# The even mixer's weight splits: low parts by an accumulating DMA onto a negated high part, instead of a VectorE subtract

## The chip, the core and the metric

The kernel runs on one core of one Trainium2 chip, as one program. The metric is the device time of one execution in microseconds (us); a lower time is better. All times here are of this one core. Engine names follow the profile: PE is TensorE (PEld its weight load), DVE VectorE, ACT ScalarE, POOL GpSimd, SP SyncE, which only issues DMAs here. A queue that an engine feeds with DMAs is written SPq, POOLq.

## The reference, cut to what matters

The program is a trunk of two layers over 512 tokens of width 1024, in fp32. Each layer is a half-step feed-forward, a mixer, an attention to 256 memory tokens and another half-step feed-forward, each followed by a layer norm. The mixer of layer 0, the even one, is what the change touches:

```python
def mixer_ab(h, w_in, w_out, q_gain, k_gain, sink, ang_2d, ang_1d):
    qa, ka, va, qb, kb, vb = jnp.split(h @ w_in, AB_SPLITS, axis=-1)   # w_in 1024 x 1536
    ...
    qa = apply_rope(rms_norm(qa, q_gain), ang_2d)
    ka = apply_rope(rms_norm(ka, k_gain), ang_2d)
    out_a = global_gqa(qa, ka, va)                       # 8 heads of 64, dense
    ...
    out_b = window_gqa_sink(qb, kb, vb, sink)            # 8 heads of 64, a band of +-128
    return jnp.concatenate([out_a, out_b], axis=-1) @ w_out            # w_out 1024 x 1024
```

The output is the (1, 512, 1024) fp32 trunk result.

## The kernel before, in words

**Products.** TensorE multiplies in fp32r, a rounded form of fp32. To keep fp32 accuracy each operand is held as two fp32r tiles: the high part is the rounded value, the low part is the value minus the high part. `mm3` (line 307) makes a product as high x high, high x low and low x high, three matmuls of 128x128 by up to 512 columns accumulated in one PSUM bank. So each weight needs a high and a low tile in SBUF before TensorE can use it.

**Weights.** `weights()` (line 313) loads up to 1 MB of fp32 weights into a `raw` buffer, of which there are two, over SyncE's DMA queue. It cuts the buffer in pieces of 128 x 1024 and for each takes two tiles of the tag `slab` (27 buffers in the kernel, shared with activations and everything else of that size). `split` (line 296) then has ScalarE copy the piece to the fp32r high tile (in the trace `ACT CAST slab<-raw`) and VectorE subtract the high tile from the piece into the low tile (`DVE TENSOR_TENSOR slab<-raw,slab`). The raw buffer comes free when both have read it.

**The even mixer** (`mixer_ab`, line 709) calls `weights()` through two helpers. `w_cols512` (line 344) fetches a group of 512 columns of `w_in` as two loads of 1 MB (512 rows each) with two pieces per load; a piece is two blocks of 128 rows by 512 columns. It is called for three groups in this order: columns 512 to 1023 (keys and values of the dense heads, half of the banded queries), 0 to 511 (dense queries) and 1024 to 1535 (the rest). That makes 12 pieces. `w_rows_pairs` (line 363) fetches rows of `w_out` for a pair of heads that lie 256 rows apart: a load has two sources, one for the lower 64 partitions and one for the upper 64. For the first half of the heads it loads half the columns at a time (4 loads with one piece each, in `half_rows`), and for the last four head pairs all columns (2 loads with two pieces each, just before `down`). That makes 8 pieces.

In time the mixer runs from about 328 us, when the first raw load is issued under the end of the first feed-forward, to about 600 us. Its stages are: layer norm of the input in four blocks of 128 tokens (VectorE, ScalarE, and on GpSimd the reciprocal root `lny`), the key and value projection (from 365 us), the query projections with RMS norm and rotary embedding (GpSimd makes the roots `rms8y`, `rms2y` and the rotary adds `slab<-t,t`), eight dense heads, eight banded heads, and the output projection, half of it mixed into the banded heads and the other half after them.

**The order of instructions.** Nearly every instruction is recorded as an operation by a `Recorder` (so nearly all carry line L143) and written out by a planner, `Graph.emit` (line 168). The planner keeps a clock per engine, gives each operation a modelled duration (`cost`, line 110), and always issues the operation that can start first; among the ready ones of an engine the one recorded first goes first. Two figures of it matter here: a GpSimd DMA is given 700 ns on its engine, and its result counts as there 4000 ns after that, plus 90 ns for any step between engines. Each engine then runs its instructions strictly in the written order. A tile's next user waits until the last reader of the buffer is done.

**An existing use of the same means.** In the feed-forward layers, `down_fast` (line 518) already makes some of its tiles by a GpSimd DMA that adds `ffn_w_down` rows from HBM onto a slab: 40 DMAs of 512 KB, in the page as `POOL DMA_DIRECT2D slab<-ffn_w_down x40`. They write plain fp32.

Of the kernel before, what the change touches and what calls it, by code (L numbers as in the profile page):

```python
# [16 lines left out]
AF = mybir.ActivationFunctionType  # L17
ALU = mybir.AluOpType
# [3 lines left out]
D = 1024  # L22
# [230 lines left out]
class Kernel:  # L253
# [56 lines left out]
        mm(ps, st[0], mv[1], start=False, stop=False, **kw)  # L310
        mm(ps, st[1], mv[0], start=False, stop=last, **kw)

    def weights(self, srcs, shape, pieces, between=None):

        nc = self.nc
        raw = self.tile(self.raw, [P, *shape], F32, "raw")
        for part, src in srcs:
            nc.sync.dma_start(out=part(raw), in_=src)
            if between:
                between()  # L320
                between = None
        got = []
        for piece in pieces:
            v = piece(raw)
            shp = list(v.shape)
            wh, wl = self.slab(F32R, shp), self.slab(F32R, shp)
            self.split(v, wh, wl)
            got.append((wh, wl))
        return got

# [13 lines left out]
    def w_cols512(self, w, c0):  # L344

        got = []
        for q in range(2):
            src = w[q * 512 : (q + 1) * 512, c0 : c0 + 512].rearrange("(k p) f -> p k f", p=P)
            got += self.weights(
                [(lambda r: r, src)], (4, 512), [lambda r, i=i: r[:, 2 * i : 2 * i + 2, :] for i in range(2)]  # L350
            )
        return got

# [9 lines left out]
    def w_rows_pairs(self, w, r0, c0=None):  # L363


        cols = slice(0, D) if c0 is None else slice(c0, c0 + 512)
        srcs = [
            (lambda r, s=s: r[64 * s : 64 * s + 64], w[r0 + 256 * s : r0 + 256 * s + P, cols].rearrange("(b p) f -> p b f", p=64))
            for s in range(2)
        ]  # L370
        if c0 is None:
            return self.weights(srcs, (2, D), [lambda r, i=i: r[:, i, :] for i in range(2)])
        return self.weights(srcs, (2, 512), [lambda r: r])[0]

    def rsqrt(self, sums, n, tag, mean, eps):

# [961 lines left out]
```

## Time and profile before

| | us |
|---|---|
| median of 3 runs | 2215.97 |
| lowest and highest of the 3 | 2215.14, 2216.75 |
| span of the profiled execution | 2218.7 |
| PE busy in it | 2185.8 (99%) |
| DVE busy in it | 1415.7 (64%) |
| ACT busy in it | 878.2 (40%) |
| POOL busy in it | 318.0 (14%) |

The profiled execution is one more run of the kernel; its span is 2.7 us longer than the median of the others. Rows of instructions read: start (us), duration (us), engine, line, operation, output tile <- inputs, size, count; a bracket at the end gives how long the engine had been idle before it and what released it. A row with a count stands for several instructions in a row. Rows of groups read: line, engine, operation, tiles, size, count, then busy us and mean ns of one, then the idle time before them and what ended it. An issue row of a DMA ends with the median time from issue to landing. GpSimd's DMA instruction is only the issue; the data lands later.

### The profile page before, as it was taken

Reading aid. Unit: us, or ns where it says so; the run is one execution under the profiler, and the core shown is the slowest. Engines: PE = TensorE matmul, PEld = TensorE weight load, DVE = VectorE, ACT = ScalarE, POOL = GpSimd, SP = SyncE. Lnnn points to the kernel's source line nnn. Section 1 sums busy time; section 2 is a strip of 40 time slices with the busy share of each in tenths; the row PEclk is TensorE's granted clock in tenths of the full one; section 3 lists DMA queues with packets and bytes.
Section 4 is the critical chain, followed back from the end, with each engine's and each line's share of the span. In section 5 each row is a group of like instructions: output and inputs, shape, how many; then the busy total and the mean of one; then the engine's idle time right before and its main releaser. Section 6 shows DMA issues by size and latency. Waiting matters only on the chain.

```text
span 2218.7 us, 28479 instructions
## 1 busy us (share of the span) xinstructions
PE 2185.8 (99%) x11264; PEld 1863.8 (84%) x11264; DVE 1415.7 (64%) x2127; ACT 878.2 (40%) x1412; POOL 318.0 (14%) x431
## 2 busy tenths in 40 slices
PE   8999999999999999999999999999999999999998
PEld 7888888778998988888888888888989989888886
DVE  5566657788745756655765566567767557566556
ACT  4333333466443433333333233245554434333331
POOL 0000022544000000000300001214330000000002
PEclk9999999999999999999999999999999999999999
DMA  7443333102442642334334444235553325433342
GB/s 222 143 142 120 106 107 104 39 10 70 130 133 96 182 135 95 95 121 149 120 105 131 143 142 147 95 102 148 141 157 124 124 96 161 124 100 93 111 152 67
DMA packets 195221, 265.15 MB, mean 120 GB/s; under 512 B 8848, under 2 KB 139536, under 8 KB 195088
## 3 DMA queue, kind: packets, MB, share of 16 engines
q1 hardware_dynamic: 181136, 231.88, 32.9%
q0 software_dynamic: 13952, 31.46, 6.6%
q8 instruction: 88, 1.44, 0.3%
q14 instruction: 45, 0.37, 0.1%
HBM read 248.63 MB, written 4.19 MB: 114 GB/s over the span
## 4 chain that ended last, share of the span: by engine, by line
PE 94%; DVE 3%; ACT 1%; POOL 1%; DMA 1%; issue 1%; SPq 0%; DVEq 0%; POOLq 0%; ACTq 0%
PE a L143 59%; PE d L143 21%; PE t L143 14%; DVE slab L143 1%; DVE t L143 1%; ACT slab L143 1%; DVE x L143 0%; POOL slab L143 0%; DMA raw<-ab_w_out 0%; ACT t L143 0%; DMA slab<-t 0%; POOL rms8y L143 0%; ACT junk L143 0%; DMA x<-x 0%; POOL lny L143 0%
## 5 line engine op out<-in xcount | busy, mean ns | idle before, releaser
L143 PE MATMUL a<-xh,slab 128*128 128x512 f32 (+1 forms) x2960 | 892.9, 382 | 0.0
L143 PEld LDWEIGHTS a<-xh,slab 128*128 128x128 f32 x2960 | 549.1, 188 | 106.8
L143 PE MATMUL a<-xl,slab 128*128 128x512 f32 (+1 forms) x1480 | 565.1, 382 | 0.0
L143 PE MATMUL d<-slab,slab 128*128 128x512 f32 (+2 forms) x1856 | 448.8, 381 | 3.3 <-ACT slab L143 3.3
L143 DVE TENSOR_TENSOR slab<-raw,slab 128x1024 fp32r<-128x1024 f32 x300 | 368.8, 1250 | 92.7 <-ACT slab L143 92.2
L143 PEld LDWEIGHTS d<-slab,slab 128*128 128x128 f32 x1856 | 334.5, 188 | 67.3 <-ACT slab L143 5.1
L143 ACT CAST slab<-raw 128x1024 fp32r<-128x1024 f32 x300 | 304.3, 1048 | 206.2 <-DMA raw<-ffn_w_gate 176.4
L143 DVE TENSOR_TENSOR slab<-slab,slab 128x1024 fp32r<-128x1024 f32 (+2 forms) x220 | 254.0, 1177 | 177.8 <-ACT slab L143 104.7
L143 PEld LDWEIGHTS a<-xl,slab 128*128 128x128 f32 x1480 | 278.3, 188 | 53.4
L143 PE MATMUL a<-slab,slab 128*128 128x256 f32 (+3 forms) x1720 | 301.2, 321 | 3.7 <-DMA slab<-t 1.4
L143 PEld LDWEIGHTS a<-slab,slab 128*128 128x128 f32 x1720 | 250.0, 190 | 31.4 <-DVE slab L143 4.6
L143 ACT ACTIVATE t<-a 128x512 f32<-128x512 f32 (+3 forms) x105 | 58.1, 554 | 525.7 <-PE a L143 525.6
L143 ACT CAST slab<-slab 128x1024 fp32r<-128x1024 f32 (+1 forms) x180 | 174.3, 1000 | 135.6 <-DVE slab L143 135.5
L143 POOL DMA_DIRECT2D slab<-ffn_w_down x40 | 48.6, 1255 | 1008.7 <-DMA slab<-ffn_w_down 639.6
L143 PE MATMUL t<-slab,slab 128*128 128x512 f32 (+1 forms) x792 | 185.4, 380 | 0.0
L143 PEld LDWEIGHTS t<-slab,slab 128*128 128x128 f32 x792 | 142.9, 188 | 29.8
L143 DVE TENSOR_TENSOR slab<-a,t 128x512 f32<-128x512 f32 x72 | 49.8, 692 | 175.7 <-PE a L143 175.7
L143 DVE TENSOR_TENSOR slab<-t,slab 128x512 fp32r<-128x512 f32 (+2 forms) x213 | 133.1, 649 | 40.0 <-ACT slab L143 39.5
L143 ACT CAST slab<-t 128x512 fp32r<-128x512 f32 (+2 forms) x213 | 114.6, 565 | 100.9 <-PE t L143 61.8
L143 DVE SCALAR_TENSOR_TENSOR x<-d,x 128x512 f32<-128x512 f32 x168 | 114.9, 686 | 47.4 <-PE d L143 46.9
L143 POOL TENSOR_TENSOR t<-t,l 128x256 f32<-128x256 f32 (+2 forms) x104 | 84.2, 831 | 344.1 <-DVE l L143 343.8
L143 PE MATMUL a<-slab,xh 128*128 128x256 f32 (+1 forms) x432 | 101.2, 328 | 2.2 <-ACT slab L143 1.6
(104 smaller groups left out, 1912.5 us busy)
## 6 DMA issues: line engine op xcount, KB each, us to landing
slab<-ffn_w_down SPq DMA_DIRECT2D x100, 512.0 KB
raw<-ffn_w_gate SPq DMA_DIRECT2D x40, 1024.0 KB
raw<-ffn_w_up SPq DMA_DIRECT2D x40, 1024.0 KB
slab<-ffn_w_down POOLq DMA_DIRECT2D x40, 512.0 KB, 9.7
slab<-t SPq DMA_DIRECT2D x96, 128.0 KB
raw<-mem_w_kv SPq DMA_DIRECT2D x8, 1024.0 KB
raw<-mem_w_kv SPq DMA_DIRECT2D x16, 512.0 KB
raw<-mem_w_q SPq DMA_DIRECT2D x8, 1024.0 KB
```

The source lines that it names most:

```text
L143: op.call = lambda: fn(*args, **kw)
```

## The change

For the pieces of `w_cols512` and `w_rows_pairs`, which only the even mixer uses, the low part is made in another way. ScalarE still copies the piece to the high tile. ScalarE then writes the negated piece, rounded to fp32r, into the low tile. GpSimd finally issues one DMA for each source of the piece, which reads the same weights again from HBM and adds them onto the low tile, leaving weight minus high part. All other weights are split as before. The planner orders the new operations with everything else.

```diff
-    def weights(self, srcs, shape, pieces, between=None):
+    def weights(self, srcs, shape, pieces, between=None, added=False):
...
             wh, wl = self.slab(F32R, shp), self.slab(F32R, shp)
-            self.split(v, wh, wl)
+            if added:
+                nc.scalar.copy(wh, v)
+                nc.scalar.activation(wl, v, AF.Copy, scale=-1.0)
+                for part, src in srcs:
+                    nc.gpsimd.dma_start(out=part(wl), in_=piece(src), accum_op=ALU.add)
+            else:
+                self.split(v, wh, wl)
             got.append((wh, wl))
...
-                [(lambda r: r, src)], (4, 512), [lambda r, i=i: r[:, 2 * i : 2 * i + 2, :] for i in range(2)]
+                [(lambda r: r, src)], (4, 512), [lambda r, i=i: r[:, 2 * i : 2 * i + 2, :] for i in range(2)], added=True
...
-            return self.weights(srcs, (2, D), [lambda r, i=i: r[:, i, :] for i in range(2)])
-        return self.weights(srcs, (2, 512), [lambda r: r])[0]
+            return self.weights(srcs, (2, D), [lambda r, i=i: r[:, i, :] for i in range(2)], added=True)
+        return self.weights(srcs, (2, 512), [lambda r: r], added=True)[0]
```

## The prediction

> **What bounds the kernel now.** I read the page's head and chain first, then its groups and DMA issues, then the windows of the even mixer (about 328 to 600 us), and last the timeline of TensorE at each place where the change moves something.
>
> ```profile
> span 2218.7 us, 28479 instructions
> PE 2185.8 (99%) x11264; PEld 1863.8 (84%) x11264; DVE 1415.7 (64%) x2127; ACT 878.2 (40%) x1412; POOL 318.0 (14%) x431
> PE 94%; DVE 3%; ACT 1%; POOL 1%; DMA 1%; issue 1%; SPq 0%; DVEq 0%; POOLq 0%; ACTq 0%
> ```
>
> TensorE is busy for 2185.8 of 2218.7 us and makes 94% of the chain that ended last. All its idle time is 32.9 us, so an edit on other engines can win at most what of that lies in the even mixer, and it loses whatever it makes TensorE wait. The profiled execution is 2.7 us over the median of the runs, 2215.97 us; I make the sum on the trace and carry only the difference over to the median. About 0.2%, or 4.4 us, is what a measurement of this kernel can tell from no change.
>
> The windows show where the mixer has slack (columns: busy us and instructions of PE, PEld, DVE, ACT, POOL; then granted clock, DMA share, GB/s):
>
> ```profile
> 347.00:365.00 18.00, 18.00 (x89) 15.02 (x88) 16.00 (x31) 8.93 (x14) 4.80 (x9) 1.00 0.32 118
> 365.00:390.00 25.00, 25.00 (x120) 20.82 (x119) 21.80 (x44) 8.04 (x16) 10.30 (x16) 1.00 0.28 90
> 390.00:420.00 30.00, 26.52 (x112) 20.55 (x110) 21.38 (x43) 10.60 (x19) 18.61 (x17) 0.94 0.22 66
> 480.00:510.00 30.00, 26.06 (x155) 21.18 (x154) 25.96 (x64) 23.59 (x54) 15.57 (x33) 1.00 0.16 36
> 540.00:570.00 30.00, 29.67 (x171) 25.69 (x170) 22.49 (x56) 17.70 (x40) 6.68 (x10) 1.00 0.51 141
> ```
>
> From 347 to 390 TensorE has no idle time although VectorE is 87 to 89% busy: VectorE's subtracts are hidden there. Idle TensorE is in two windows, 3.5 us at 390 to 420 (with the clock at 0.94) and 3.9 us at 480 to 510. Only there can a freed VectorE pay.
>
> **What goes and what comes.** The rows that price it:
>
> ```profile
> L143 DVE TENSOR_TENSOR slab<-raw,slab 128x1024 fp32r<-128x1024 f32 x300 | 368.8, 1250 | 92.7 <-ACT slab L143 92.2
> L143 ACT CAST slab<-raw 128x1024 fp32r<-128x1024 f32 x300 | 304.3, 1048 | 206.2 <-DMA raw<-ffn_w_gate 176.4
> L143 POOL DMA_DIRECT2D slab<-ffn_w_down x40: 1194/1203/1699, 28.8 to 2121.4; - x40
> DMA to landing us min/median/max: 6.1/9.7/12.5
> slab<-ln_g POOLq DMA_DIRECT2D x8, 512.0 KB, 4.1
> ```
>
> Twenty pieces change. VectorE loses 20 subtracts of 1.25 us, 25 us. ScalarE gains 20 negated copies; I price them as the cast of the same shape, 1.05 us, 21 us. GpSimd gains 28 issues: 12 of 512 KB for the input projection (one each), and 16 of 256 KB for the output projection (two each, one per half of the partitions). A 512 KB issue holds GpSimd for 1.2 us; for the smaller ones I take 0.6 us, half the rows. The low part of a piece was ready one subtract after its cast, about 2.3 us; now it is ready after cast, negation, issue and landing. The nearest rows for the landing are 40 accumulating 512 KB DMAs of the feed-forward layers: 6.1 to 12.5 us, median 9.7. Those come in pairs beside heavy loads; a plain 512 KB DMA of the same queue takes 4.1. The mixer's windows move 66 to 141 GB/s, so I take the low end, 6.1, as the likely value (for 256 KB too, since no row shows a discount) and keep 4.1 to 12.5. So: hidden where the planner issues early, late where it cannot. Whether these accumulate into fp32r at the same speed as into plain fp32, no row shows.
>
> The Trainium skill, page "DMA: Bandwidth & Descriptors", section "Anatomy of one DMA — SWDGE (gpsimd) path", fits a GpSimd-issued DMA as 2.0 us plus bytes over 436 GB/s; for 512 KB that makes an estimate of 3.2 us, and by it the two landing terms below would be zero. The trace differs (6.1 at the least for accumulation), so I do not use it.
>
> **Step by step**, with positions from the changed program's instruction order and times walked from rows of the trace.
>
> *First projection (keys and values).* TensorE starts it here and uses the four lows up to about 369.3:
>
> ```profile
> 353.12 1.99 ACT L143 CAST slab<-raw 128x1024 fp32r<-128x1024 f32 x2
> 358.03 2.00 ACT L143 CAST slab<-raw 128x1024 fp32r<-128x1024 f32 x2
> 364.96 0.62 PE L143 MATMUL a<-slab,xh 128*128 128x512 f32 x2
> 357.27 0.42 POOL L143 TENSOR_SCALAR lny<-var 128x1 f32<-128x1 f32 x1 [3.11 <-ACT junk L143]
> ```
>
> The lows' DMAs are issued at about 338.5, 344, 355 and 359.3, the last two behind the layer norm's GpSimd steps (the row at 357.27). The last is needed at 369.3, ten us after its issue: no stall at 6.1 or 9.7, 2.0 at 12. I take +0.3. The raw buffer is now released by ScalarE alone, so the next load of 1 MB comes earlier, and the next group's lows are in time. Two of these issues, 1.2 us each, stand ahead of the layer norm's reciprocal root of later token blocks; TensorE waits on those blocks with little to spare: 0 to +0.5, I take +0.3.
>
> *The q and k rotary bubble.* TensorE's largest stall of the mixer:
>
> ```profile
> 391.94 1.65 POOL L143 TENSOR_TENSOR rms8y<-rms8y,nhalf 128x8 f32<-128x8 f32 x1
> 395.79 2.37 POOL L143 TENSOR_TENSOR slab<-t,t 128x512 f32<-128x512 f32 x1 [2.20 <-DVE t L143]
> 410.19 1.28 POOL L143 TENSOR_TENSOR slab<-t,t 128x512 f32<-128x512 f32 x1 [2.26 <-PE a L143]
> 395.82 3.41 DVE L143 TENSOR_TENSOR slab<-raw,slab 128x1024 fp32r<-128x1024 f32 x2
> 398.21 0.47 PE L143 MATMUL t<-ident,slab 128*128 128x128 f32 x1 [2.02 <-POOL slab L143]
> 398.33 1.20 PE L143 MATMUL a<-slab,xh 128*128 128x512 f32 x2
> 402.42 0.39 PE L143 MATMUL a<-slab,xl 128*128 128x512 f32 x1
> 411.52 0.33 PE L143 MATMUL t<-ident,slab 128*128 128x128 f32 x1 [0.53 <-POOL slab L143]
> 417.87 0.33 PE L143 MATMUL t<-ident,slab 128*128 128x128 f32 x1 [0.75 <-POOL slab L143]
> ```
>
> GpSimd's rotary add takes 2.37 us beside VectorE's two subtracts and 1.28 without them; TensorE waits 2.02 us and then runs about 3.4 us at half pace (a pair in 1.20 us against 0.62 later), which costs another 1.7. The Trainium skill, page "SBUF — State Buffer", on who interferes with whom, says a VectorE operation with two SBUF inputs locks out a GpSimd one that reads SBUF; the pair 2.37 and 1.28 agrees. The subtracts go, which saves up to 1.1, and the chain ahead of it on VectorE starts some 1.6 earlier; but a DMA issue of 1.2 us now stands on GpSimd between the root at 391.94 and this add, and another before the add for the next keys, where a new stall of about 1 opens. The later stalls, 0.53 and 0.75, become 0.5 to 1.0 and about 0.1. If the first stall falls below what dropped the clock, the 1.7 go as well. Ends -3.5 and +1; I take -1.0, since the issues give back most of what the subtracts free.
>
> *Third group's last low.* ScalarE reaches its negation only behind work for the first queries; issued at 411 to 414, it lands at 417 to 420 by 6.1 and at 421 to 424 by 9.7. TensorE asks at 419 to 424: 0 to 1, up to 3 at 9.7 or more; I take +0.5.
>
> *480 to 510.* Both VectorE and ScalarE are nearly full here, and what TensorE waits for last is ScalarE:
>
> ```profile
> PE d L143 <- ACT slab L143: 2.9, 3, 1.1
> 488.87 0.50 PE L143 MATMUL d<-slab,slab 128*128 128x512 f32 x1 [0.81 <-ACT slab L143]
> 498.95 0.51 PE L143 MATMUL d<-slab,slab 128*128 128x512 f32 x1 [1.00 <-ACT slab L143]
> 505.21 1.19 PE L143 MATMUL d<-slab,slab 128*128 128x256 f32 x3 [1.13 <-ACT slab L143]
> ```
>
> Four negations (4.2 us in all) lie in and around this window and four subtracts leave. ScalarE's casts there wait on transposes that themselves wait on VectorE's softmax, so part comes back: -0.5 to +1.5, I take +0.3.
>
> *The end of the output projection.* The last four pieces leave the least lead:
>
> ```profile
> 554.90 2.01 ACT L143 CAST slab<-raw 128x1024 fp32r<-128x1024 f32 x2
> 560.11 1.05 ACT L143 CAST slab<-raw 128x1024 fp32r<-128x1024 f32 x1 [1.88 <-DMA raw<-ab_w_out]
> 562.83 0.59 ACT L143 CAST slab<-d 128x512 fp32r<-128x512 f32 x1 [0.46 <-PE d L143]
> 563.10 2.23 PE L143 MATMUL a<-slab,slab 128*128 128x512 f32 x9
> 565.18 2.88 PE L143 MATMUL d<-slab,slab 128*128 128x512 f32 x12
> ```
>
> Each cast is followed by its negation, so the negations end at about 557.0, 560.7, 563.4 and 565.4 (the third and fourth wait for the load at 560.11 and stand behind the cast at 562.83). In the new order, TensorE goes through the pieces one after another over several banks, 12 matmuls or 2.7 us a piece, and asks for the lows at 563.9, 566.9, 569.4 and 571.2. The last has 5.8 us, 5.2 after its second issue. Landing in 4.1: no stall; 6.1: 0.9; 9.7: 4.5; 12.5: 7.3, and a stall of two or more also pays the 1.7 of half pace. The window moves 141 GB/s, between the others and the feed-forward's; I take 6.1 with a little for GpSimd: +1.2.
>
> The sum: 0.3 + 0.3 - 1.0 + 0.5 + 0.3 + 1.2 = +1.6 us, a span of 2220.3 and a median of 2217.6. From 600 us on both programs are the same and TensorE bound, so it passes to the end undiminished.
>
> **The rivals.**
> *Late landings decide (slower).* The accumulations land as in the feed-forward layers, at 9.7. For it: that is the median of 40 alike, and the mixer's end also loads the next weights (141 GB/s). Against: those come as pairs under heavier load. If accumulating into fp32r is slower than into fp32, it is this case too. At 9.7: 4.5 + 1.7 at the end, +1.5 for the third group, the other terms at 0.9 - 1.0: +7.6, or 2223.6; at 12, some +14. It decides beyond 4.4 us from a landing of about 8. Chance 0.30.
> *The bubble closes (faster).* Rotary add and half pace both go: -3.5, with the last stalls at 417 and 480 to 510 shrinking by another 1 to 2 as VectorE frees 25 us, and landings at 4.1 hidden: -5, or 2211. Against it stand the GpSimd issues in the same chain. Chance 0.13.
> *ScalarE binds at 480 to 510.* All four negations push the casts that TensorE waits for: +4.2, plus 1.6 from the rest, 2221.8. For: 2.9 us of waits on it already. Against: 6.4 us free in that window. Chance 0.07.
>
> **How the numbers follow.** My forecast, near +1.6, keeps 0.50. Of the slower rival's 0.30 nearly all is beyond 0.2%, of ScalarE's half. Faster by over 0.2%: 0.14. Within: 0.50. Slower: 0.36. The range runs from the closed bubble, 2211.5, to late landings at about 11 us, 2227, and leaves out some 2 in 10; the forecast's own range is 2212.5 to 2221.
>
> **What would show it.** Right: landings of the DMAs into the slabs from the mixer's weights near 6 us, TensorE waiting on them under 2.5 us in all, the row at 398 with a stall of 0.5 to 1.5, 365 to 390 still without idle, 480 to 510 within 1.5 us of its 26.06. Wrong: landings of 8 us or more with idle TensorE before 575, or a clock below 1.00 in a window that had it full.

## The result, and the profile after

The changed kernel took 2223.89 us (median of 6 runs, 2223.19 to 2226.08) against 2216.61 us of the kernel before in the same comparison (6 runs): a ratio of 1.0032 with a 95% interval of 1.0021 to 1.0043, so 7 us slower, beyond the 0.2% that I had set as the limit. It lies inside the stated range, and on the side of the slower rival, not of the forecast.

The head of the page after, and the share of the chain that ended last:

```profile
span 2224.2 us, 28559 instructions
PE 2187.5 (98%) x11264; PEld 1863.7 (84%) x11264; DVE 1389.6 (62%) x2107; ACT 897.5 (40%) x1432; POOL 340.0 (15%) x459
PE 91%; DVE 2%; ACT 2%; POOL 2%; DMA 1%; issue 1%; SPq 0%; POOLq 0%; DVEq 0%; ACTq 0%
```

The engines' totals moved much as priced (25, 21 and 24 us): VectorE lost 26.1 us, ScalarE gained 19.3, GpSimd 22.0. The price of a single issue was off: two of the 256 KB issues in a row hold GpSimd for 1.63 to 1.71 us at the end, where the prediction had 1.2. None of that is the time lost. The windows of the mixer, in the columns of the prediction's windows, tell where it went:

```profile
347.00:365.00 18.00, 17.19 (x84) 14.01 (x83) 15.02 (x28) 12.24 (x17) 7.42 (x11) 1.00 0.89 234
365.00:390.00 25.00, 24.79 (x118) 20.44 (x118) 15.83 (x45) 10.44 (x19) 15.05 (x21) 1.00 0.83 195
390.00:420.00 30.00, 27.50 (x124) 21.54 (x123) 15.97 (x38) 15.99 (x26) 18.48 (x19) 1.00 0.57 105
480.00:510.00 30.00, 27.27 (x160) 22.02 (x158) 24.03 (x67) 25.33 (x58) 16.84 (x37) 1.00 0.34 72
540.00:570.00 30.00, 25.59 (x147) 21.99 (x146) 14.25 (x35) 18.00 (x36) 12.34 (x17) 0.95 0.70 163
```

TensorE is busier where it was idle (390 to 420 and 480 to 510) and idle where it was not: 4.4 us at 540 to 570, with the clock below 1.00. Two GpSimd loads for the next layer norm are the same in both programs and mark the time before and after the end of the output projection. Of before, then of after:

```profile
546.73 0.66 POOL L143 DMA_DIRECT2D slab<-ln_g  x1
682.88 0.63 POOL L143 DMA_DIRECT2D slab<-ln_g  x1 [6.68 <-PE a L143]
```

```profile
544.36 0.63 POOL L143 DMA_DIRECT2D slab<-ln_g  x1
687.53 0.64 POOL L143 DMA_DIRECT2D slab<-ln_g  x1 [6.69 <-PE a L143]
```

The changed kernel is 2.4 us ahead at the first mark and 4.65 us behind at the second, so the stretch between them, 136.15 us before, is 7.0 longer. From there on the distance stays near 4.65 to the last layer norm. The two spans differ by 5.5 and the medians by 7.3; that remainder lies in parts where the programs are alike, and one trace of each doesn't place it.

TensorE's rows at the end of the output projection, and what it waited for:

```profile
561.45 0.93 PE L143 MATMUL d<-slab,slab 128*128 128x512 f32 x3 [0.45 <-DMA slab<-ab_w_out]
568.64 1.62 PE L143 MATMUL d<-slab,slab 128*128 128x512 f32 x3 [3.96 <-DMA slab<-ab_w_out]
570.06 1.48 PE L143 MATMUL a<-slab,slab 128*128 128x512 f32 x3
571.34 1.48 PE L143 MATMUL d<-slab,slab 128*128 128x512 f32 x3
572.62 1.05 PE L143 MATMUL a<-slab,slab 128*128 128x512 f32 x2
573.47 0.96 PE L143 MATMUL d<-slab,slab 128*128 128x512 f32 x3
```

A wait of 0.45 and one of 3.96 us on the DMAs of the low parts, then 11 matmuls from 568.64 to 573.47 in 4.8 us, where at full clock (0.227 us apart) they take 2.5. That is 4.4 + 2.3 = 6.7 of the 7.0 us.

### The profile page after: what moved, and what is told of

It reads as the page before. It is cut to its first block, busy times and chain, and to the rows that moved or that the text cites. A ratio compares the mean times of both kernels' runs of the same rounds, so it can differ in the third digit from the quotient of the medians.

```text
span 2224.2 us, 28559 instructions
## 1 busy us (share of the span) xinstructions
PE 2187.5 (98%) x11264; PEld 1863.7 (84%) x11264; DVE 1389.6 (62%) x2107; ACT 897.5 (40%) x1432; POOL 340.0 (15%) x459
## 4 chain that ended last, share of the span: by engine, by line
PE 91%; DVE 2%; ACT 2%; POOL 2%; DMA 1%; issue 1%; SPq 0%; POOLq 0%; DVEq 0%; ACTq 0%
PE a L143 57%; PE d L143 21%; PE t L143 13%; ACT slab L143 1%; DVE slab L143 1%; DVE t L143 1%; DMA slab<-t 1%; DVE x L143 1%; DMA slab<-ab_w_out 0%; POOL slab L143 0%; SPq L143 0%; POOL lny L143 0%; ACT junk L143 0%; POOL t L143 0%; ACT t L143 0%
## 5 line engine op out<-in xcount | busy, mean ns | idle before, releaser
L143 DVE TENSOR_TENSOR slab<-raw,slab 128x1024 fp32r<-128x1024 f32 x280 | 342.1, 1242 | 101.4 <-ACT slab L143 101.0
```

The lines of the kernel that those rows point to most:

```text
L143: op.call = lambda: fn(*args, **kw)
```

## The experiments

**The last four pieces alone.** First the change without its last four pieces, then the last four pieces without the rest.

```diff
 # e1_tail_by_vector, from the changed kernel
-            return self.weights(srcs, (2, D), [lambda r, i=i: r[:, i, :] for i in range(2)], added=True)
+            return self.weights(srcs, (2, D), [lambda r, i=i: r[:, i, :] for i in range(2)])
 # e2_tail_only, from the changed kernel
-                [(lambda r: r, src)], (4, 512), [lambda r, i=i: r[:, 2 * i : 2 * i + 2, :] for i in range(2)], added=True
+                [(lambda r: r, src)], (4, 512), [lambda r, i=i: r[:, 2 * i : 2 * i + 2, :] for i in range(2)], added=False
-        return self.weights(srcs, (2, 512), [lambda r: r], added=True)[0]
+        return self.weights(srcs, (2, 512), [lambda r: r])[0]
```

> Only the last four pieces of w_out (the two 1 MB loads ahead of the final down) are split by VectorE again; the other 16 pieces keep the accumulating DMA. Theory (the loss is all in the last four pieces, the rest is a gain): no wait of TensorE on a DMA at 555 to 575, the 2.2 us that the changed kernel had won by 546 us are kept, about 2214.4, 2 us faster than before. Rival (the earlier gain is only borrowed, from a later start of the last pieces' casts): it falls back to 2216 to 2217 at the end.

> Only the last four pieces of w_out are made by the accumulating DMA; the 16 others are split by VectorE as before. Theory (the last four alone cost it): stall of 4 to 5 us on the DMA and some 2 us at half clock, about 2223.5, 7 us slower than before. Rival (the late landing comes from what the earlier pieces changed): 2217 to 2219.

A ratio here is an estimate over the runs and not the quotient of the two medians, from which it differs by up to 0.0005. Without the last four: 2215.05 us against 2218.47, ratio 0.9988 (0.9979 to 0.9997), faster than both kernels. With them alone: 2225.99, ratio 1.0039 (1.0025 to 1.0053). In the first, TensorE waits on no DMA between 540 and 620; in the second its row is

```profile
571.91 1.62 PE L143 MATMUL d<-slab,slab 128*128 128x512 f32 x3 [5.04 <-DMA slab<-ab_w_out]
```

So the loss is all in the last four pieces, it needs nothing of the rest, and the rest is a gain that is kept.

**Why they land late.** The view of the DMA queues from 558 to 569 us, in the kernel before and then in the changed one (queue: packets, MB, share of the 16 engines; below, issues with the median time to landing):

```profile
DMA packets 2126, 2.21 MB, mean 201 GB/s; under 512 B 60, under 2 KB 2100, under 8 KB 2124
q1 hardware_dynamic: 2124, 2.19, 65.8%
```

```profile
DMA packets 1405, 2.29 MB, mean 208 GB/s; under 512 B 76, under 2 KB 1103, under 8 KB 1405
q0 software_dynamic: 370, 1.24, 61.2%
q1 hardware_dynamic: 1035, 1.05, 31.7%
slab<-ab_w_out POOLq DMA_DIRECT2D x6, 256.0 KB, 9.9
raw<-mem_w_kv SPq DMA_DIRECT2D x1, 1024.0 KB
raw<-mem_w_kv SPq DMA_DIRECT2D x2, 512.0 KB
```

The engines are 93% taken, by six accumulating DMAs and the three loads of `mem_w_kv`, weights of the stage that follows, together. SyncE issued those loads here, before and after:

```profile
561.10 4.00 SPq L143 DMA_DIRECT2D raw<-mem_w_kv  x3
```

```profile
557.93 5.84 SPq L143 DMA_DIRECT2D raw<-mem_w_kv  x3
```

They come 3.2 us earlier (2.4 of it since the whole program is ahead), just as the last six accumulations are issued, at 558.19 to 563.4. That they come earlier is not what matters: in the kernel with the last four pieces alone (e2) they start here, only 0.45 us earlier than before, and the wait is longer, 5.04 us.

```profile
560.65 5.71 SPq L143 DMA_DIRECT2D raw<-mem_w_kv  x3
```

Three theories: the loads compete (A), eight accumulations in a row delay each other (B), accumulating itself is slow (C). The next two test them.

```diff
 # e3_loads_held, from the changed kernel (self.held collects the raw buffers)
         ws = [z for b in range(2) for z in self.w_rows_pairs(w_out, 512 + 128 * b)]
+        for raw in self.held[-2:]:
+            nc.gpsimd.tensor_tensor(
+                out=raw[:, 0, 0:8], in0=ws[-1][1][:, 0:8].bitcast(F32), in1=self.nhalf, op=ALU.mult
+            )
 # e5_plain_dma, from the changed kernel
-                    nc.gpsimd.dma_start(out=part(wl), in_=piece(src), accum_op=ALU.add)
+                    nc.gpsimd.dma_start(out=part(wl), in_=piece(src))
```

> As the changed kernel, but the next loads into the two raw buffers (mem_w_kv) may start only when the last low part has landed: a small GpSimd operation reads that low part and writes a corner of each raw buffer. Theory A (the low parts land late because the mem_w_kv loads, which start at 557.9, share the DMA engines with them): the last six landings fall from 8.9 to 11.2 us to 5 to 7, the wait of 4.0 us to under 1.5, the half clock goes, and the time falls by 4 to 6 us to 2218 to 2220, if the later loads are not missed. Theory B (eight accumulating DMAs back to back delay each other): landings stay at 9 to 11 and so does the wait, 2224 or more.

> As the changed kernel with the same 28 DMAs, but without adding: they overwrite the low tile with the weights (so the low parts are wrong; time only). Theory C (accumulating itself is what takes long): landings at light load fall from 6 us to about 4, at the end from 9 to 11 to under 6, no wait, about 2215. Theories A and B: at the end the landings stay within 1 to 2 us of the changed kernel's and TensorE still waits 2 to 4 us, 2221 to 2224.

With the loads held to 571 us: 2222.15 us, ratio 1.0019 (1.0010 to 1.0028). The same view of 558 to 569, and TensorE's waits:

```profile
q0 software_dynamic: 534, 1.77, 99.5%
slab<-ab_w_out POOLq DMA_DIRECT2D x6, 256.0 KB, 6.5
```

```profile
565.42 0.93 PE L143 MATMUL d<-slab,slab 128*128 128x512 f32 x3 [1.36 <-DMA slab<-ab_w_out]
570.77 0.70 PE L143 MATMUL d<-slab,slab 128*128 128x512 f32 x2 [0.41 <-DMA slab<-ab_w_out]
587.91 1.07 PE L143 MATMUL t<-ident,x 128*128 128x128 f32 x8 [1.08 <-DVE x L143]
```

The median landing falls from 9.9 to 6.5 us, the long wait from 3.96 to 1.36 and the half clock is gone: for the landings and the waits the loads are the larger part (A). But the accumulations alone still fill the engines, at 99.5% for 1.77 MB in 11 us, where SyncE's plain loads moved 2.19 MB at 65.8% in the kernel before: for a MB, an accumulation takes 1.9 times the engines' time. So they queue behind each other, which is B's share, and a wait remains. Waits of 1.1 and 0.6 us then appear at 588 to 590, behind VectorE, so the expected 4 to 6 us were only partly had.

Without adding: 2222.29 us, ratio 1.0016 (1.0007 to 1.0025). In the projections the landings of the 12 DMAs fall from 5.8 at the least and 7.6 in the median to:

```profile
L143 POOL DMA_DIRECT2D slab<-ab_w_in x12: 713/768/813, 338.3 to 411.4; - x12
DMA to landing us min/median/max: 4.0/5.5/8.5
```

So accumulating costs about 2 us of landing and 0.5 us of GpSimd's issue (1.23 in the changed kernel). On the same queue and with little beside it, the first of these DMAs took 56.5% of the engines for its 6.04 us in the changed kernel and 51.0% for its 3.97 us here, for the same 0.52 MB: 1.7 times, so most of the 1.9 is the adding itself. At the end the last six landings still take 6.8 to 9.3 us, some 2 us less each than in the changed kernel, where the held loads took off some 3.5. TensorE still waits 3.1 us, with the clock at 0.81 from 566 to 575: for the waits C is real and the smaller part.

The times do not rank the two. Between the two `ln_g` loads the kernel with held loads takes 140.6 us and the one without adding 140.9, against 143.2 of the change and 136.15 before, and their ratios are 1.0019 and 1.0016. Each gives back 2.3 to 2.6 of the 7.0 us, and no run has both.

**Reading from SBUF, telling the planner, fewer DMAs.**

```diff
 # e11_from_raw
+                    nc.gpsimd.dma_start(out=part(wl), in_=part(v), accum_op=ALU.add)
 # e6_planner_told: the planner counts 9500 ns from the issue to the landing of these DMAs
+                    nc.ops[-1].land = 9500.0
 # e12_one_dma_a_piece: one source pattern over both halves, last four pieces
+                bass.AP(v.tensor, v.offset, [[256 * D, 2], [D, 64], [1, D]])
```

> As the changed kernel, but each accumulating DMA reads the piece from the raw buffer in SBUF instead of HBM. The raw buffers are then held until the low parts have landed, so the mem_w_kv loads start only after them, and 10 MB less are read from HBM. Theory A (the low parts wait behind the mem_w_kv loads): the last landings come down to 5 to 7.5 us as with held loads, the wait of 4.0 us to under 1.5, about 4 us faster than the changed kernel (ratio to before 1.000 to 1.002). Theory D (the second read of HBM itself delays them): lower still, under 5 us, ratio under 1.000. Rival: the raw buffers held in the projections delay the loads there and TensorE waits on those, ratio 1.002 or more.

> As the changed kernel, but the planner counts 9.5 us instead of 4.0 from the issue of these DMAs to their landing. If the stall at the end is a matter of order (TensorE had other work that the planner would have put ahead, had it known), the wait on DMA falls to 1 to 2 us and the ratio to before to 1.000 to 1.002. If nothing else was ready (the last four pieces close the mixer), TensorE waits as long as before, ratio 1.003.

> As the changed kernel, but the last four pieces take one accumulating DMA of 512 KB over 128 partitions each instead of two of 256 KB over 64. Theory A (bytes in competition decide, not the number of DMAs): the last landings stay within 1 us of the second halves' 9.8 to 11.2, TensorE waits 3 to 4.5 us, ratio 1.002 to 1.004. Theory B (the number of DMAs in a row decides): landings under 8, wait under 2, ratio under 1.002.

From the raw buffer: 2222.77 us, ratio 1.0019 (1.0009 to 1.0028). It holds the raw buffers by itself, and the loads start at 564.8; the last six land in 6.3 to 9.2 us, no better than with held loads, so the second read of HBM is not what delays them there (D falls). With little beside it, the source does count: the first of these DMAs lands in 4.6 us, in the changed kernel in 6.04. TensorE waits on all four pieces, 3.7 us in all with 1.9 the longest, more than A alone had let expect. By the `ln_g` load near 545 it is 3.1 us ahead of before, so the rival (loads delayed in the projections) does not show; from there to the next `ln_g` load it loses 8.5 us.

With the planner told: 2223.38 us, ratio 1.0024 (1.0015 to 1.0034), not to be told from the changed kernel. TensorE's one wait on these DMAs is 3.5 us: the order has little else to put there.

With one DMA a piece: 2238.41 us, ratio 1.0087 (1.0070 to 1.0103), far outside what either theory expected.

```profile
581.97 1.22 PE L143 MATMUL a<-slab,slab 128*128 128x512 f32 x2 [21.78 <-DMA slab<-ab_w_out]
slab<-ab_w_out POOLq DMA_DIRECT2D x4, 512.0 KB, 26.9
```

Its question, number or bytes, stays open, since the pattern changed something larger. From 566 to 581 us the four DMAs hold `q0 software_dynamic` at 48.1% of the engines, half of them. The Trainium skill, page "DMA: Bandwidth & Descriptors", section "Why a DMA increments its semaphore by 16 and not by 1", says that a DMA is spread over the largest number of engines up to 16 that divides the slowest dimension of both patterns. Here these are 2 and 128, which makes an estimate of 2 engines each and at most 8 for four; the 48.1% agrees. In the changed kernel the slowest dimension is 64 rows. This is not a proof: the same view has 553 packets under 512 B, against 76 in the changed kernel's from 558 to 569, and no run has the same DMA with another outermost dimension.

**Where the gain is from.** Each group by itself, and the two that gain together:

```diff
 # e4_third_group_only and e10_third_and_halves, in w_cols512
-    for i in range(2)], added=True
+    for i in range(2)], added=c0 == 1024
 # e9_first_groups_only, in w_cols512
-    for i in range(2)], added=True
+    for i in range(2)], added=c0 != 1024
```

In e8 no piece of `w_cols512` is added; in e4 and e9 none of `w_rows_pairs` is, in e8 and e10 only the pieces of `half_rows`.

> Only the third group of w_in (columns 1024 to 1535, four pieces, whose two subtracts stand beside the rotary add at 395.8) uses the accumulating DMA; all else is split by VectorE. Theory (the gain of the first part comes from taking these subtracts away from the rotary add, which closes the stall of 2.0 us and the half clock behind it): the stall at 398 falls under 0.5, the clock of 390 to 420 is 1.00, and the program is 2.5 to 3.5 us ahead at 420 and 2 to 3 us faster at the end, about 2214. Rival (the gain comes from the second group, which leaves VectorE earlier, or from the output pieces at 480 to 510): within 1 us of before.

> Only the first and second group of w_in (eight pieces) use the accumulating DMA. Theory: the small stalls of 1.0 us in all that the changed kernel has between 347 and 376 appear, the stall at 398 stays at 1.5 to 2.0 with the half clock, so 0.5 to 1.5 us slower than before, 2217 to 2218. Rival (freeing VectorE before 390 is what closes the stall): 2 us faster.

> Only the four pieces of w_out that half_rows loads (the first half of the heads) use the accumulating DMA. Theory (ScalarE takes on what VectorE loses at 480 to 510): TensorE's idle time there goes from 3.9 to about 2.7 us as in the changed kernel, so 0.5 to 1.2 us faster. Rival (the four negations make ScalarE, on which TensorE waited for 2.9 us there, later): 1 to 3 us slower.

> The third group of w_in and the half_rows pieces by the accumulating DMA, the first two groups and the last four pieces by VectorE. If the parts add up: the gain of the third group and of the halves without the 1.0 us of small stalls at 347 to 376, 3 to 4 us faster than before, the fastest so far, about 2213. Rival (each new order makes its own stalls, so parts do not add): between the two alone, 2214 to 2216.

| kernel | ratio to before | 95% interval | from the `ln_b` load near 329 to the `ln_g` load near 545, against before's 217.3 us |
|---|---|---|---|
| the change | 1.0032 | 1.0021 to 1.0043 | -2.2 |
| all but the last four (e1) | 0.9988 | 0.9979 to 0.9997 | -2.6 |
| third group only (e4) | 0.9998 | 0.9990 to 1.0007 | -1.8 |
| first two groups only (e9) | 0.9999 | 0.9990 to 1.0008 | -0.7 |
| halves only (e8) | 0.9998 | 0.9989 to 1.0007 | -2.2 |
| third group and halves (e10) | 0.9988 | 0.9979 to 0.9997 | -3.1 |

Alone none of the three can be told from before by its time; together, 2214.68 against 2218.54 us, they can, and they match the version without the last four. The 2 to 3 us expected of the third group alone, the 0.5 to 1.2 of the halves and the small loss of the first two groups were not seen in their times; only the traces order them, and one trace of each is thin for less than a microsecond: the change, e1, e3 and e12 differ only after 545 us in what was edited, and give -2.2 to -2.6. The third group's mechanism shows in the rows. GpSimd's rotary add near 395 in the changed kernel, with the issue ahead of it:

```profile
393.46 1.25 POOL L143 DMA_DIRECT2D slab<-ab_w_in  x1
395.72 1.28 POOL L143 TENSOR_TENSOR slab<-t,t 128x512 f32<-128x512 f32 x1 [1.01 <-DVE t L143]
```

and in e9, where VectorE's subtracts of the third group still stand beside it, and in e4, where they are gone:

```profile
395.22 2.18 POOL L143 TENSOR_TENSOR slab<-t,t 128x512 f32<-128x512 f32 x1 [2.20 <-DVE t L143]
397.45 0.33 PE L143 MATMUL t<-ident,slab 128*128 128x128 f32 x1 [1.53 <-POOL slab L143]
```

```profile
396.09 1.26 POOL L143 TENSOR_TENSOR slab<-t,t 128x512 f32<-128x512 f32 x1 [0.99 <-DVE t L143]
397.40 0.33 PE L143 MATMUL t<-ident,slab 128*128 128x128 f32 x1 [0.94 <-POOL slab L143]
```

The add is 0.9 us shorter with the subtracts gone, and in both DMA versions it still waits 1.0 us for VectorE after the issue: the issue sits in idle time. The stall of 2.02 us becomes 1.53 in e9 and 0.94 in e4, where under 0.5 was expected, and 0.19 only with both in the changed kernel; TensorE's waits from 390 to 425 add up to 4.4 us before, 3.8 in e9, 3.7 in e4 and 2.7 in the changed kernel. So the first two groups help here about as much as the third. For the halves, 480 to 510 shows TensorE busy for 27.41 us in e8 against 26.06 before.

The half clock after the first stall is not fixed. In e8, where all up to 450 us is as before, TensorE has the same stall and no half clock after it (two matmuls in 0.71 us, before 1.20), and by 487 us it is 1.1 us ahead with nothing changed until then, so half of its -2.2 in the table is not the halves' doing. In e9 too the half clock is absent, against what was expected:

```profile
398.63 0.33 PE L143 MATMUL t<-ident,slab 128*128 128x128 f32 x1 [2.02 <-POOL slab L143]
398.71 0.71 PE L143 MATMUL a<-slab,xh 128*128 128x512 f32 x2
```

## Why the prediction was right or wrong

The range and the side of the slower rival hold; the forecast of +1.6 does not, and both signs that the prediction named for being wrong are there: landings of 8 us or more with TensorE idle before 575 us, and a clock of 0.95 at 540 to 570, which had 1.00 before.

*First projection, +0.3 and +0.3: 1.0 measured, for another reason in part.* TensorE never waited on these DMAs (they landed in 5.8 to 10.9 us). The wait of 0.21 us at 374 is the layer norm's, as expected. The larger one, 0.81 us at 350.14, is not in the prediction: VectorE, in order, waited for a small load that landed late, with the DMA share at 0.61 instead of 0.45 in that window (328 to 347), and the subtract that TensorE needed stood behind it. VectorE waits for this load in e9 too (1.4 us), and not in e4, e8 or e10, so it comes with the first two groups.

```profile
349.04 0.45 DVE L143 TENSOR_SCALAR nsink<-nsink 128x8 f32<-128x8 f32 x1 [1.42 <-DMA nsink<-ab_sink]
349.40 0.68 DVE L143 TENSOR_TENSOR slab<-t,slab 128x512 fp32r<-128x512 f32 x1
350.14 0.50 PE L143 MATMUL d<-slab,slab 128*128 128x512 f32 x1 [0.81 <-DVE slab L143]
```

*The rotary bubble, -1.0 (to -3.5): about -2.3.* TensorE's transposes of 487.41 start at 486.00, 1.3 earlier counted from the loads near 329, in spite of the 1.0 lost before. The stall of 2.02 became 0.19, and the half clock went, for which e8 gives 1.1 rather than my 1.7. The step "the issues give back most of what the subtracts free" failed: the issue fills time in which the add waits for VectorE anyway. The new stall of about 1 for the next keys was 0.26; the later two, 0.53 and 0.75, became 0.92 and nothing.

*Third group's last low, +0.5: nothing.* Issued at 412.26, landed 7.91 us later, no wait.

*480 to 510, +0.3: about -1.0.* The idle time there went from 3.9 to 2.7 us, in e8 as in the change, and some comes back by 540. ScalarE is fuller (25.33 us against 23.59) and TensorE waits less on it, so I read the earlier waits as VectorE's delay passed on; no run separates the two.

*The end, +1.2: +7.0.* This is the term that decided. The landing was taken as 6.1 us, "with a little for GpSimd", from a window of 141 GB/s; the last six took 8.9 to 11.2. A mean over 30 us hid that the next loads, of `mem_w_kv`, start in just these microseconds, before as after (561.10 and 557.93). The prediction's price for a landing of 9.7 us, 4.5 + 1.7, stands beside 4.4 + 2.3, but only in part for its reason. It put the stall at the last piece. In the trace the long wait is for the second, whose later DMA was issued at 558.71 and landed 9.79 us later, at 568.50; the last two pieces landed by 571.48 and 574.62, while TensorE was behind and at half clock, and it did not wait for them. The rival's total, +7.6, is close to +7.3 in part by chance, since it held +1.5 for the third group and nothing for the halves.

## What to carry to other kernels

A step that moves work from an engine to a DMA should be made only where its result is wanted later than the landing under load, and that load includes the loads of the next stage that run there and the change's own DMAs, which held the engines 1.7 times as long per MB as plain ones: read the landing from the loaded rows, at the place, not from a window's mean. Split such a change by place and keep the parts that have slack; here 8 pieces (third group and halves) give the same gain as 16, and the last 4 cost more than twice that gain. When a DMA takes the place of an instruction on an engine, look at the small loads too: here one landed late beside the new DMAs, and cost TensorE 0.81 us.

## What the runs showed of the hardware

- An accumulating DMA into fp32r takes 5.7 to 6.1 us to land for 512 KB when little competes, a plain one 4.0 to 4.2; the issue takes 1.23 against 0.77 us. Per MB it holds the DMA engines 1.7 times as long as a plain DMA of the same queue (e5), and 1.9 times as long as SyncE's plain loads by the two queue views from 558 to 569 us.
- One DMA of 512 KB whose source has an outermost dimension of 2 landed in 25.9 to 28.5 us.
- After a stall of TensorE of 2.02 us the clock was halved for some 3.4 us in the kernel before (0.66 at 398 to 403, and the same in e2 after 2.04 us), and not in e8. The Trainium skill, page "TensorE: Matmul & The Clock Gate", section "What's actually happening", describes a free-running activity window, so that how many matmuls run slow varies from run to run; the two traces agree with that. It sets the drop after at least one idle window of about 3.4 us; here 2.02 us were enough.
